# Token loads moved into the first half of layer 0's modulation weights, and small loads moved off the SP queue

## The chip, the cores and the metric

The kernel runs on one core of a Trainium2 chip. TensorE (PE) multiplies matrices, VectorE (DVE) and ScalarE (ACT) do elementwise work, GpSimd (POOL) does a few tiny operations, and SyncE (SP) issues most of the loads. Each engine works through its own list of instructions strictly in order. The metric is the time of one execution in microseconds on the device; less is better.

## The reference

Two transformer layers over 256 latent tokens `x` and 256 context tokens `ctx`, each of width 1024. Before each sub-layer a token row is normed and then modulated by vectors that come from a conditioning vector (`c` for latents, `c_ctx` for context):

```
mod_x = silu(c) @ ada_w[l] + ada_b[l]          # 6 * 1024 columns: shift, scale, gate, twice
hx    = modulate(rmsnorm(x, mix_pre_g[l]), shift, scale)
zx    = hx @ w_in[l]                           # then four mixing branches, SwiGLU, residuals
```

All is float32; a product is made in three passes of split operands. Nothing of the main work can start before the modulated tokens `hx`, `hc` of layer 0 are there, and these need both the normed tokens and `silu(c) @ ada_w[0]` for shift and scale (8 MB of weights).

## The kernel before

**The head.** `run` (L1114) starts with `setup`: it loads `c`, `c_ctx` and an identity matrix and makes `cs = silu(c)`. Then `ada_first` (L269) computes shift (j = 0) and scale (j = 1) of layer 0 for both streams. Its weights come as 16 loads of 512 KB, all issued by SP. The output columns are taken in two halves h (512 columns each), and within a half in pairs of k (128 rows of the contraction each); so a half is eight loads. The product over k is shared: all of j = 1 and the last k of j = 0 go to PE as `g<-ada,cs` (L301, 2 output rows by 512 columns, each recorded as two matmuls), the first `CUT` = 3 or 6 k of j = 0 go to DVE, which accumulates `acc` for both streams by `scalar_tensor_tensor` (L101). DVE then transposes `acc` in blocks (L332), sums the blocks to `vsum` (L333), and PE folds the four quarters (L339). ACT copies PE's rows out (`row`), PE transposes them, and DVE adds all up into the columns `adac`. The generator yields at its two ends of half.

**The tokens.** `load_x` brings `x` and `ctx` in as four loads of 512 KB. The table entry `XPOS` says after which (h, k) of the weights' loads they are issued: (1, 0), so after ten weight loads. For each of the four tiles of 128 tokens ACT squares the two halves of a row (`xs<-x`, with sums), DVE and POOL make the reciprocal root (`vn`, `rn`), and DVE scales the row, 512 columns at a time (`normed`, L413). PE transposes 128x128 blocks (`a<-ident,xs`, L179), and `modulated` (L431) applies shift and scale (`hm`) and splits the result in two parts, `h` on ACT and the rest on DVE. That is done for output half h = 0 first (k tiles 0 to 3), then for h = 1.

**What follows.** The first product of the main work is `g<-wh,h` (L170 to L172) with a unit of `w_in`, whose weights are split into `wh` (ACT) and `wl` (DVE). From then on the weights stream in by units.

**What sets the order.** The instructions are written by these generators, and a scheduler of the language then lays them in each engine's list; a wait holds everything behind it on that engine. Loads issued by SP and ACT take eight completion semaphores in turn, and a load that takes one again first waits for the load that had it; POOL's loads have eight others.

**The small loads.** `vectors(l)` (L212) loads eight vectors of a layer (`vin`, 85 rows of 128 numbers), issued by SP: for layer 0 after the fourth weight load, for layer 1 after the tables. `tables` (L231) loads the rotary tables `r` and the mask `mf` (320 KB), also by SP. `layer_consts` loads `gk`, `sink` and `wpl` by POOL.

Of the kernel before, what the change touches and what calls it, by code (L numbers as in the profile page):

```python
# [33 lines left out]
FILL = (2.0, 1.8)  # L34
RATE = (0.3, 0.45, 0.9, 1.0, 0.5)
CUT = (3, 6)
XPOS = (1, 0)
PUMP = ((0, 20, 2.5, 2.5, 7.5, 15), (15, 0, 30, 20, 2.5, 0))
NEG = -1e30

# [31 lines left out]
class Backbone:  # L72
# [138 lines left out]

    def vectors(self, l):  # L212

        d, c, g = self.d, self.const, self.nc.sync.dma_start
        vin = self.tp.tile([85, 128], F, tag=f"vin{l}", name="vin")
        row = lambda a: a[l].rearrange("(k p) -> k p", p=128)
        at = 0
        for name in ("mix_pre_g", "ffn_pre_g", "ada_b", "d_scale", "b_qa_g", "b_kva_g", "mix_post_g", "ffn_post_g"):
            r = row(d[name])
            g(vin[at:at + r.shape[0]], r)  # L220
            at += r.shape[0]
        yield
        ps = self.pa()
        self.tr(ps[:, 0:85], vin)
        col = c.tile([128, 85], F, tag=f"cols{l}", name="cols")
        self.act(col, ps[:, 0:85])
        self.cols[l] = dict(mix=col[:, 0:8], ffn=col[:, 8:16], ada=col[:, 16:64], ds=col[:, 64:66],
                            qa=col[:, 66:68], kva=col[:, 68:69], mixp=col[:, 69:77], ffnp=col[:, 77:85])
        yield

    def tables(self):  # L231
        nc, d, c, g = self.nc, self.d, self.const, self.nc.sync.dma_start
        t = lambda shape, name, dt=F: c.tile(shape, dt, name=name, tag=name)
        self.r64, self.r32 = t([128, 2, 128], "r64"), t([128, 2, 64], "r32")
        g(self.r64, d["rope64"])
        g(self.r32, d["rope32"])
        mf = self.tp.tile([128, 2, 128], F, tag="mf", name="mf")
        g(mf, d["mask"])
        self.mask, self.identb = t([128, 2, 128], "mask", BF), t([128, 128], "identb", BF)
        nc.vector.tensor_copy(self.mask, mf)  # L240
        nc.vector.tensor_copy(self.identb, self.ident)
# [27 lines left out]
    def ada_first(self, load, vec):  # L269


        w = self.d["ada_w"][0].rearrange("(k p) n -> p k n", p=128)
        raw = {}
        for h in range(2):
            for k in range(0, NK, 2):
                for j in range(2):
                    t = self.tp.tile([128, 2, 512], F, tag="ada", name="ada", bufs=16)
                    self.nc.sync.dma_start(t, w[:, k:k + 2, j * D + h * 512:j * D + h * 512 + 512])
                    raw[j, h, k], raw[j, h, k + 1] = t[:, 0], t[:, 1]
                if h == 0 and k == 2:  # L280
                    next(vec)
                if (h, k) == XPOS:
                    load()
        for j in range(2):
            for s in range(2):
                self.mod[0, j, s] = self.const.tile([128, NK], F, tag=f"ada0{j}{s}", name="adac")
        def add(j, h, x, y):
            c = slice(4 * h, 4 * h + 4)
            for s in range(2):
                o = self.mod[0, j, s][:, c]  # L290
                self.tt(o, x[:, :, s], o if y is None else y[:, c], ALU.add)

        v = self.vsums()
        for h in range(2):
            cut = (CUT[h], 0)
            ps = [self.pg() for j in range(2)]
            acc = [self.ap_.tile([128, 512], F, tag="acc", name="acc", bufs=2) for s in range(2)]
            for k in range(NK):
                for j in range(2):
                    if k >= cut[j]:  # L300
                        self.nc.tensor.matmul(ps[j][0:2], self.cs[:, :, k], raw[j, h, k], start=k == cut[j], stop=k == NK - 1)  # L301
                    else:
                        for s in range(2):
                            self.ada_step(acc[s], raw[j, h, k], s, k, self.ts)
            if h == 0:
                next(vec)
            for s in range(2):
                self.quad_sums(v[:, s, 16 * h:16 * h + 16], acc[s], raw[0, h, s])
            pv = self.pg()
            self.fold_quads(pv, v[:, :, 16 * h:16 * h + 16])  # L310
            add(0, h, pv[:, 0:8].rearrange("p (s k) -> p k s", s=2), self.cols[0]["ada"])
            for j in range(2):
                row = self.tp.tile([128, 512], F, tag="row", name="row", bufs=4)
                self.act(row[0:2], ps[j][0:2])
                x = pv[:, 8 + 8 * j:16 + 8 * j].rearrange("p (k s) -> p k s", s=2)
                for k in range(4):
                    self.tr(x[:, k], row[0:2, k * 128:(k + 1) * 128])
                add(j, h, x, self.cols[0]["ada"][:, NK:2 * NK] if j else None)
            yield
# [90 lines left out]
        return out  # L410


    def normed(self, x, ss, out):  # L413

        v = self.sm(1, "vn")
        self.ts(v, ss[:, 0:1], ss[:, 1:2], EPS, ALU.add, ALU.add)
        r = self.pow_half(v, 1, "n")
        for h in range(2):
            c = slice(h * 512, h * 512 + 512)
            self.ts(out[:, c], x[:, c], r)  # L420

    def turn_in(self, t, x, pss, ks):

# [423 lines left out]
    def mixer(self, l, xs, hs, streams):  # L847
        tc = self.tc
        with ExitStack() as st:
# [40 lines left out]
            def pump(t):  # L890
                run([t])
# [222 lines left out]
    def run(self):  # L1114
        tc = self.tc
        self.mod = {}
        xs, both = {}, (0, 1)
# [6 lines left out]
        with tc.tile_pool(name="start", bufs=1) as self.tp:  # L1124
            self.setup()
            self.cols = {}
            vec = [self.vectors(l) for l in range(LAYERS)]
            tmp = {s: [self.tp.tile([128, D], F, tag="xs", name="xs", bufs=4) for _ in range(2)] for s in both}
            first = self.ada_first(lambda: xs.update({s: self.load_x(s, self.nc.sync) for s in both}), vec[0])
            next(first)  # L1130
            for s in both:
                for t in range(2):
                    self.normed(xs[s][t], self.squares(xs[s][t], tmp[s][t]), tmp[s][t])
            next(first)
            for h in range(2):
                for s in both:
                    ab = self.ab(0, "mix", s, (slice(4 * h, 4 * h + 4),))
                    pss = {}
                    for t in range(2):
                        self.turn_in(t, tmp[s][t], pss, (4 * h, 4 * h + 2))  # L1140
                    self.modulated(s, pss, ab, self.H)
                if not h:
                    self.first_w = self.wunit(self.d["w_in"][0], C_U, 256)
            self.tables()
            self.layer_consts(0)
            for _ in vec[1]:
                pass
# [57 lines left out]
```

## Time and profile before

| | us |
|---|---|
| median of 3 runs | 1337.62 (1335.01 to 1339.58) |
| the profiled execution, its own time | 1333.19 |
| its span, first to last instruction | 1331.4 |
| PE busy in the span | 1282.5 (96%) |
| DVE busy | 988.6 (74%) |
| ACT busy | 681.7 (51%) |

The span and the 1.8 us around it make the execution's own time. Times in the rows count from the start of the span. A row of the timeline gives start, duration, engine, line, operation, output and inputs, and in brackets how long the engine had idled before it and what ended that. Rows of matmuls that follow each other closely overlap: a duration holds the way through the array, so the distance of two starts is what one costs.

### The profile page before, as it was taken

Reading aid. Unit: us, or ns where it says so; the run is one execution under the profiler, and the core shown is the slowest. Engines: PE = TensorE matmul, PEld = TensorE weight load, DVE = VectorE, ACT = ScalarE, POOL = GpSimd, SP = SyncE. Lnnn points to the kernel's source line nnn. Section 1 sums busy time; section 2 is a strip of 40 time slices with the busy share of each in tenths; the row PEclk is TensorE's granted clock in tenths of the full one; section 3 lists DMA queues with packets and bytes.
Section 4 is the critical chain, followed back from the end, with each engine's and each line's share of the span. In section 5 each row is a group of like instructions: output and inputs, shape, how many; then the busy total and the mean of one; then the engine's idle time right before and its main releaser. Section 6 shows DMA issues by size and latency. Waiting matters only on the chain.

```text
span 1331.4 us, 20465 instructions
## 1 busy us (share of the span) xinstructions
PE 1282.5 (96%) x7357; PEld 1086.9 (82%) x7357; DVE 988.6 (74%) x2114; ACT 681.7 (51%) x1553; POOL 48.7 (4%) x74
## 2 busy tenths in 40 slices
PE   5998999999999999999999999989899999999997
PEld 1777787888778878887788888889799998798996
DVE  4867688878999668888557664676887888785664
ACT  2545466646655535343244333454766667545552
POOL 1012000000000010000000000110000000000000
PEclk9999999999999999999999999999999999999999
DMA  8734432243244714565547553055332536577652
GB/s 291 235 110 115 127 87 64 69 138 94 74 127 154 250 48 134 183 190 167 173 151 220 167 174 119 22 169 175 96 111 72 151 111 213 161 244 214 179 178 87
DMA packets 150521, 194.50 MB, mean 146 GB/s; under 512 B 6682, under 2 KB 106324, under 8 KB 150164
## 3 DMA queue, kind: packets, MB, share of 16 engines
q1 hardware_dynamic: 149092, 188.73, 45.7%
q0 software_dynamic: 1312, 4.46, 1.2%
q8 instruction: 58, 0.95, 0.3%
q14 instruction: 43, 0.35, 0.1%
q10 hardware_dynamic: 16, 0.00, 0.0%
HBM read 192.12 MB, written 1.05 MB: 145 GB/s over the span
## 4 chain that ended last, share of the span: by engine, by line
PE 78%; DVE 7%; DMA 7%; ACT 4%; issue 2%; POOL 1%; SPq 0%; DVEq 0%; POOLq 0%; ACTq 0%
PE g L170 20%; PE g L171 20%; PE g L172 20%; DMA araw<-in_ada_w_dram 4%; PE a L179 3%; PE a L170 3%; PE a L172 3%; PE a L171 3%; PE a L652 2%; PE a L601 2%; DVE acc L101 2%; DVE wl L93 2%; ACT grp L90 1%; DVE grp L93 1%; DMA ada<-in_ada_w_dram 1%
## 5 line engine op out<-in xcount | busy, mean ns | idle before, releaser
L90 ACT ACTIVATE wh<-raw 128x512 fp32r<-128x512 f32 (+1 forms) x482 | 296.7, 626 | 312.5 <-PE g L171 167.0
L93 DVE TENSOR_TENSOR wl<-raw,wh 128x512 fp32r<-128x512 f32 (+1 forms) x482 | 323.8, 684 | 119.9 <-ACT wh L90 117.3
L170 PE MATMUL g<-h,wh 128*128 128x512 f32 (+1 forms) x1168 | 394.0, 338 | 3.9 <-ACT th L90 1.3
L171 PE MATMUL g<-h,wh 128*128 128x512 f32 (+1 forms) x1168 | 392.8, 337 | 0.0
L172 PE MATMUL g<-h,wl 128*128 128x512 f32 (+1 forms) x1168 | 392.3, 336 | 0.0
L170 PEld LDWEIGHTS g<-h,wh 128*128 128x128 f32 x1168 | 221.0, 190 | 28.4 <-ACT th L90 1.8
L172 PEld LDWEIGHTS g<-h,wl 128*128 128x128 f32 x1168 | 221.5, 190 | 21.6
L171 PEld LDWEIGHTS g<-h,wh 128*128 128x128 f32 x1168 | 221.5, 190 | 21.2 <-issue 0.4
L101 DVE SCALAR_TENSOR_TENSOR acc<-araw,cs,acc 128x512 f32<-128x512 f32 x224 | 162.1, 748 | 89.5 <-DMA araw<-in_ada_w_dram 67.1
L170 PE MATMUL g<-wh,h 128*128 128x256 f32 (+3 forms) x368 | 111.8, 305 | 1.7 <-ACT h L90 1.7
L172 PE MATMUL g<-wh,h 128*128 128x256 f32 (+3 forms) x368 | 111.0, 303 | 2.5 <-DVE h L93 2.5
L171 PE MATMUL g<-wl,h 128*128 128x256 f32 (+3 forms) x368 | 111.2, 303 | 0.5 <-DVE wl L93 0.5
L101 DVE SCALAR_TENSOR_TENSOR th<-th,g 128x512 f32<-128x512 f32 (+1 forms) x126 | 67.8, 559 | 11.1 <-PE g L172 6.8
L172 PEld LDWEIGHTS g<-wh,h 128*128 128x128 f32 x368 | 70.3, 191 | 4.4 <-DVE h L93 2.9
L170 PEld LDWEIGHTS g<-wh,h 128*128 128x128 f32 x368 | 70.3, 191 | 4.2 <-ACT h L90 2.2
L171 PEld LDWEIGHTS g<-wl,h 128*128 128x128 f32 x368 | 70.3, 191 | 2.3 <-DVE wl L93 0.7
L90 ACT ACTIVATE th<-g 128x512 f32<-128x512 f32 (+1 forms) x102 | 49.8, 492 | 38.0 <-PE g L172 37.3
L90 ACT ACTIVATE p<-a,nm 128x512 f32<-128x512 f32 (+1 forms) x72 | 44.2, 614 | 23.0 <-DVE nm L97 17.3
L170 PE MATMUL a<-wh,g 128*128 128x512 f32 x132 | 52.6, 399 | 1.1 <-DVE adac L93 1.1
L172 PE MATMUL a<-wh,g 128*128 128x512 f32 x132 | 52.2, 395 | 0.0
L171 PE MATMUL a<-wl,g 128*128 128x512 f32 x132 | 52.0, 394 | 0.0
L90 ACT ACTIVATE pth<-a 128x512 fp32r<-128x512 f32 (+1 forms) x72 | 37.8, 525 | 25.0 <-PE a L179 24.3
(228 smaller groups left out, 2000.9 us busy)
## 6 DMA issues: line engine op xcount, KB each, us to landing
raw<-in_w_ffn_dram SPq DMA_DIRECT2D x128, 512.0 KB
raw<-in_w_in_dram SPq DMA_DIRECT2D x84, 512.0 KB
araw<-in_ada_w_dram SPq DMA_DIRECT2D x80, 512.0 KB
ada<-in_ada_w_dram SPq DMA_DIRECT2D x16, 512.0 KB
raw<-in_w_branch_dram SPq DMA_DIRECT2D x32, 256.0 KB
raw<-in_w_out_dram SPq DMA_DIRECT2D x16, 512.0 KB
raw<-in_w_in_dram SPq DMA_DIRECT2D x8, 416.0 KB
band<-in_pool_dram POOLq DMA_DIRECT2D x2, 1024.0 KB, 7.9
```

What stands on the lines that cost most here:

```text
L90: return self.nc.scalar.activation(out, in_, func, **k)
L93: return self.nc.vector.tensor_tensor(out=out, in0=a, in1=b, op=op)
L101: return self.nc.vector.scalar_tensor_tensor(out=out, in0=a, scalar=s, in1=b, op0=op0, op1=op1)
L170: mm(ps, ah, bh, start=k == 0 and opens, stop=False, skip_group_check=True)
L171: mm(ps, ah, bl, start=False, stop=False, skip_group_check=True)
L172: mm(ps, al, bh, start=False, stop=last, skip_group_check=True)
L179: self.nc.tensor.transpose(out, in_, self.ident[0:k, 0:k])
L601: nc.tensor.matmul(ps[:, 0:nk], x, y, start=i == 0, stop=i == len(mms) - 1 and not masked)
L652: nc.tensor.matmul(po[:, 0:256], grp[:, 4, kts[k] * 128:kts[k] * 128 + 128], pt[j][:, k], start=j == 0 and k == 0, stop=j == 1 and k == n - 1)
```

## The change

`XPOS` becomes (0, 4): the tokens are loaded after six of the sixteen weight loads. `vectors` issues its loads from ACT for layer 0 and from POOL for layer 1, and is started before the first weight load; its transposed block takes a PSUM buffer of the other pool. `tables` issues its loads from POOL. `ada_first` yields once more, right after issuing its loads, and `run` now writes the four norms before the first half's products, and all transposes of a half before its last sums. In `normed` the second half of a row is scaled by ACT.

```diff
-XPOS = (1, 0)
+XPOS = (0, 4)
...
     def vectors(self, l):
-        d, c, g = self.d, self.const, self.nc.sync.dma_start
+        d, c, g = self.d, self.const, (self.nc.gpsimd if l else self.nc.scalar).dma_start
...
-        ps = self.pa()
+        ps = self.pg()
...
     def tables(self):
-        nc, d, c, g = self.nc, self.d, self.const, self.nc.sync.dma_start
+        nc, d, c, g = self.nc, self.d, self.const, self.nc.gpsimd.dma_start
...
     def ada_first(self, load, vec):
+        next(vec)
         for h in range(2):
...
-                if h == 0 and k == 2:
-                    next(vec)
                 if (h, k) == XPOS:
                     load()
+        yield
...
-    def normed(self, x, ss, out):
+    def normed(self, x, ss, out, by_act=()):
...
-            self.ts(out[:, c], x[:, c], r)
+            if h in by_act:
+                self.act(out[:, c], x[:, c], scale=r)
+            else:
+                self.ts(out[:, c], x[:, c], r)
...
-                    self.normed(xs[s][t], self.squares(xs[s][t], tmp[s][t]), tmp[s][t])
-            next(first)
+                    self.normed(xs[s][t], self.squares(xs[s][t], tmp[s][t]), tmp[s][t], (1,))
             for h in range(2):
+                pss = {s: {} for s in both}
                 for s in both:
-                    ab = self.ab(0, "mix", s, (slice(4 * h, 4 * h + 4),))
-                    pss = {}
                     for t in range(2):
-                        self.turn_in(t, tmp[s][t], pss, (4 * h, 4 * h + 2))
-                    self.modulated(s, pss, ab, self.H)
+                        self.turn_in(t, tmp[s][t], pss[s], (4 * h, 4 * h + 2))
+                next(first)
+                for s in both:
+                    self.modulated(s, pss[s], self.ab(0, "mix", s, (slice(4 * h, 4 * h + 4),)), self.H)
```

What this makes of the engines' lists is shown at three places; behind the first 150 or so rows of PE the lists are the same but for line numbers.

SP, from the first weight load to the token loads (`ada` are weights of shift and scale, `vin` the small vectors, `x` the tokens), before:

```order
L278 DMA ada<-in_ada_w_dram 128x2x512 x4
L220 DMA vin<-in_mix_pre_g_dram 8x128
L220 DMA vin<-in_ffn_pre_g_dram 8x128
L220 DMA vin<-in_ada_b_dram 48x128
L220 DMA vin<-in_d_scale_dram 2x128
L220 DMA vin<-in_b_qa_g_dram 2x128
L220 DMA vin<-in_b_kva_g_dram 1x128
L220 DMA vin<-in_mix_post_g_dram 8x128
L220 DMA vin<-in_ffn_post_g_dram 8x128
L278 DMA ada<-in_ada_w_dram 128x2x512 x6
L1021 DMA x<-in_x_dram 128x1024 x2
```

and of the changed kernel, from its first row on:

```order
L193 DMA cin<-in_c_dram 8x128
L195 DMA ident<-in_ident_dram 128x128
L279 DMA ada<-in_ada_w_dram 128x2x512 x6
L1024 DMA x<-in_x_dram 128x1024 x2
L1024 DMA x<-in_ctx_dram 128x1024 x2
L279 DMA ada<-in_ada_w_dram 128x2x512 x10
L132 DMA raw<-in_w_in_dram 128x4x256 x4
```

The `vin` rows have left SP's list, the tokens stand four loads earlier, and `w_in`'s units follow the weights without anything between.

DVE at the end of the second half's sums (`acc` up to `vsum`; `h` and `hm` are modulated tokens, `wl` split weights of `w_in`), before:

```order
L101 SCALAR_TENSOR_TENSOR acc<-ada,cs,acc 128x512
L97 TENSOR_SCALAR xs<-x,rn 128x512 x2
L101 SCALAR_TENSOR_TENSOR acc<-ada,cs,acc 128x512 x7
L332 STREAM_TRANSPOSE ada<-acc 128x512 x2
L333 TENSOR_REDUCE vsum<-ada 128x16 x2
L93 TENSOR_TENSOR h<-hm,h 128x256 x3
L98 TENSOR_SCALAR hm<-a,adac 128x256 x2
```

and of the changed kernel:

```order
L101 SCALAR_TENSOR_TENSOR acc<-ada,cs,acc 128x512
L93 TENSOR_TENSOR h<-hm,h 128x256 x2
L98 TENSOR_SCALAR hm<-a,adac 128x256
L101 SCALAR_TENSOR_TENSOR acc<-ada,cs,acc 128x512
L93 TENSOR_TENSOR h<-hm,h 128x256
L101 SCALAR_TENSOR_TENSOR acc<-ada,cs,acc 128x512 x3
L332 STREAM_TRANSPOSE ada<-acc 128x512
L93 TENSOR_TENSOR wl<-raw,wh 128x512 x2
L333 TENSOR_REDUCE vsum<-ada 128x16
L93 TENSOR_TENSOR wl<-raw,wh 128x512 x2
L332 STREAM_TRANSPOSE ada<-acc 128x512
L93 TENSOR_TENSOR wl<-raw,wh 128x512
```

The last `vsum` comes right behind these rows. Before, the modulation of the first half stood behind it, but for one `hm`; now all of that modulation (four `hm`, eight `h`) and five `wl` stand ahead of it.

PE from the token transposes to the first products of the main work, before:

```order
L179 MATMUL a<-ident,xs 128x128 x20
L301 MATMUL g<-ada,cs 2x512 x8
L339 MATMUL g<-vsum,quads 32x8 x4
L179 MATMUL a<-ident,xs 128x128 x4
L170 MATMUL g<-wh,h 128x256
L179 MATMUL a<-ident,xs 128x128 x2
L179 MATMUL g<-ident,row 128x2 x4
```

and of the changed kernel:

```order
L301 MATMUL g<-ada,cs 2x512 x2
L179 MATMUL a<-ident,xs 128x128 x4
L301 MATMUL g<-ada,cs 2x512 x3
L339 MATMUL g<-vsum,quads 32x8 x4
L179 MATMUL g<-ident,vin 128x85
L170 MATMUL g<-wh,h 128x256
L171 MATMUL g<-wl,h 128x256
L172 MATMUL g<-wh,h 128x256
L179 MATMUL g<-ident,row 128x2 x4
```

In both lists the fold of the second half (L339) stands ahead of the first `g<-wh,h`; the token transposes that stood behind the fold have moved ahead of it.

## Rows read from the trace of the kernel before

**Rows 1.** The page: busy time of the engines, share of the span and instructions
```profile
PE 1282.5 (96%) x7357; PEld 1086.9 (82%) x7357; DVE 988.6 (74%) x2114; ACT 681.7 (51%) x1553; POOL 48.7 (4%) x74
```
**Rows 2.** Windows: stretch, length, busy by engine, granted clock, DMA share, GB/s
```profile
10.00:16.00 6.00, 5.83 (x10) 0.92 (x10) 5.70 (x11) 0.00 (x0) 0.00 (x0) 1.00 0.46 147
18.00:34.00 16.00, 12.59 (x44) 4.39 (x41) 7.51 (x24) 8.34 (x23) 2.65 (x4) 0.88 1.04 410
38.00:44.00 6.00, 6.00 (x28) 1.96 (x27) 6.00 (x14) 2.45 (x6) 0.00 (x0) 1.00 0.60 162
50.00:60.00 10.00, 10.00 (x86) 10.00 (x86) 9.27 (x23) 9.50 (x25) 1.58 (x3) 1.00 0.57 165
```
**Rows 3.** Timeline of SP: the last small load and the next weights
```profile
13.21 0.27 SPq L220 DMA_DIRECT2D vin<-in_ffn_post_g_dram  x1
13.52 3.09 SPq L278 DMA_DIRECT2D ada<-in_ada_w_dram  x6
```
**Rows 4.** Timeline of ACT: the first square of tile 0 and of tile 1
```profile
25.38 0.63 ACT L90 ACTIVATE xs<-x 128x512 f32<-128x512 f32 x1 [0.24 <-DMA x<-in_x_dram]
...
26.66 0.63 ACT L90 ACTIVATE xs<-x 128x512 f32<-128x512 f32 x1
```
**Rows 5.** Timeline of DVE: second half's sums, and what stands between
```profile
22.80 0.88 DVE L97 TENSOR_SCALAR acc<-ada,cs 128x512 f32<-128x512 f32 x2 [5.17 <-DMA ada<-in_ada_w_dram]
24.89 0.23 DVE L93 TENSOR_TENSOR adac<-g,adac 128x4 f32<-128x4 f32 x2 [1.20 <-PE g L179]
...
27.64 0.88 DVE L97 TENSOR_SCALAR xs<-x,rn 128x512 f32<-128x512 f32 x2 [0.68 <-POOL rn L117]
...
33.54 0.88 DVE L97 TENSOR_SCALAR xs<-x,rn 128x512 f32<-128x512 f32 x2 [0.44 <-POOL rn L117]
34.34 4.72 DVE L101 SCALAR_TENSOR_TENSOR acc<-ada,cs,acc 128x512 f32<-128x512 f32 x7
38.98 1.30 DVE L332 STREAM_TRANSPOSE ada<-acc 128x512 f32<-128x512 f32 x2
40.20 1.24 DVE L333 TENSOR_REDUCE vsum<-ada 128x16 f32<-128x512 f32 x2
41.35 1.09 DVE L93 TENSOR_TENSOR h<-hm,h 128x256 fp32r<-128x256 f32 x3
42.35 1.00 DVE L98 TENSOR_SCALAR hm<-a,adac 128x256 f32<-128x256 f32 x2
...
55.50 1.29 DVE L93 TENSOR_TENSOR wl<-raw,wh 128x512 fp32r<-128x512 f32 x2
```
**Rows 6.** Timeline of PE in the head
```profile
17.48 7.03 PE L301 MATMUL g<-ada,cs 128*2 128x512 f32 x16 [0.39 <-DMA ada<-in_ada_w_dram]
...
25.57 1.88 PE L301 MATMUL g<-ada,cs 128*2 128x512 f32 x4
...
35.13 7.47 PE L301 MATMUL g<-ada,cs 128*2 128x512 f32 x15
42.01 0.24 PE L339 MATMUL g<-vsum,quads 128*32 128x8 f32 x6
...
47.70 0.60 PE L179 MATMUL a<-ident,xs 128*128 128x128 f32 x4
```
**Rows 7.** Windows of PE: stretch, length, PE busy, granted clock, DMA share, GB/s
```profile
30.00:31.00 1.00, 0.79 (x4) 0.54 1.05 406
...
36.00:37.00 1.00, 1.00 (x3) 0.54 1.09 388
...
122.00:123.00 1.00, 0.71 (x2) 0.62 0.97 268
...
125.00:126.00 1.00, 0.43 (x2) 0.67 0.84 263
```
**Rows 8.** DMA issues: size, us from issue to landing
```profile
gk<-in_a_kn_g_dram POOLq DMA_DIRECT2D x1, 32.0 KB, 6.9
sink<-in_c_sink_dram POOLq DMA_DIRECT2D x1, 2.0 KB, 7.8
```

## The prediction

> **What bounds the kernel now.** I read the page first: PE is busy 96% of the span [rows 1], so a change pays only where PE waits, or where it stands in front of PE's work. The change touches the head alone, so the windows came next. From 50 us on PE is busy without a gap, at the full clock [rows 2]; from there on a delay or a gain of the head moves everything behind it by the same amount, since the engines' lists behind the head are the same. Two windows show holes in the transfers: the DMA share is 0.46 from 10 to 16 and 0.60 from 38 to 44, against 1.04 and 410 GB/s between [rows 2]. The first hole is (1 - 0.46) x 6 = 3.2 us, and SP's timeline says why: the next weights are issued at 13.52, behind a `vin` row that was held until 13.21 [rows 3]. The second is (1 - 0.60) x 6 = 2.4 us.
>
> Then the engines' timelines of the head. The main work opens with `g<-wh,h`, and ahead of it in PE's list stands the fold of the second half's sums, at 42.01 [rows 6]. It waits for DVE's last `vsum`, which ends at 40.20 + 1.24 = 41.44 [rows 5]. From 34.34 on DVE goes from `acc` through the transposes to `vsum` without a gap [rows 5]. So DVE's list sets the start of the main work, and the reader should ask of the change: when does DVE reach that last `vsum`?
>
> **The change part by part.**
>
> *Transfers.* A 512 KB load takes 524 KB / 410 GB/s = 1.28 us [rows 2]. Before, the first tokens are the eleventh such load and ACT starts on them at 25.38 [rows 4]. Now they are the seventh: 4 x 1.28 = 5.1 earlier. The `vin` loads no longer hold SP: 3.2 earlier. The 320 KB of tables now run beside the first weights instead of behind them: 0.8 later at 410 GB/s. So the tokens begin at 25.4 - 5.1 - 3.2 + 0.8 = 17.9. The first half's last weights, the twelfth load, land at 17.9 + 5 x 1.28 = 24.3, the second half's first at 25.6, and the last at 34.5 instead of 36.9. The units of `w_in` follow at once, so the second hole goes too; but PE has its data then anyway, so that is worth nothing.
>
> *Norms.* Two squares cost ACT 26.66 - 25.38 = 1.28 per tile [rows 4]. ACT's half of the scaling isn't in the trace; DVE's half row takes 0.44 [rows 5], a square of that shape 0.63 [rows 4], I take 0.55. Four tiles make 4 x 1.83 = 7.3, and the last one's root adds the 27.64 - 26.66 = 1.0 that tile 0 shows [rows 4, 5]. The norms end near 17.9 + 7.3 + 1.0 = 26.2; ACT's part could move this by 0.4 either way.
>
> *DVE up to the last `vsum`.* The second half's `acc` now stand behind the norms: they start at 26.2, not at 22.80, though their data are there at 25.6. From there DVE's list holds: two first `acc` 0.88; ten more at 4.72 / 7 = 0.67, 6.7; three pairs of `adac` at 0.23, 0.7; four `hm` at 0.50, 2.0; eight `h` at 1.09 / 3, 2.9; two transposes 1.3; two sums 1.24; five `wl` at 0.645, 3.2 [rows 5]. That is 19.0. It also waits for the first half's columns from PE; before, that wait was 1.2 [rows 5], and I take the same, between 0 and the 5.2 that the first `acc` pair shows as a wait for data. So `vsum` ends at 26.2 + 19.0 + 1.2 = 46.4, against 41.44: **5.0 later**. The data that now come early do not help, since the work that filled the space behind the fold (`h`, `hm`, `wl`) has moved ahead of it.
>
> *PE behind the fold.* Twelve of the token transposes stood behind the fold and now stand ahead of it, in time in which PE waits: 3 x 0.60 = **1.8 earlier** [rows 6]. The modulation of the second half and its weights must be ready for PE's second 48 products; they have 48 x 10 / 86 = 5.6 us for it [rows 2], and before, with more of DVE's work left, PE had no gap in 50 to 60 [rows 2]. No cost.
>
> *The clock.* Before, the last four matmuls of the first product group start at 25.57 [rows 6]; then PE only transposes tokens, and the granted clock falls in the window 30 to 31 (0.54, so at 30.1) from 2.4 to 1.2 GHz. It is back in the window 36 to 37 (at 36.9) [rows 7], after products began again at 35.13 [rows 6]. Now the same stretch of transposes comes in the midst of the first half: the products of load six end near 18.3 (its data at 16.6, two products of 2 x 0.43 each), and the next stand behind the third tile's transposes, near 24.5. So I expect the fall there. The four products that follow are eight matmuls of 0.43 at full clock [rows 6] and 0.86 at half, and DVE waits for their columns: 0.9 lost if the clock returns as it did (15 matmuls took 7.47 where 16 took 7.03 [rows 6]), 3.4 if it does not. I take half of the eight: **1.7 later**. Then PE's last product ends near 40 and it idles until the fold at 46: the main work begins at half clock. The rows have 0.9 for such a return (the one above) and 1.7 (3.4 us at half between the windows 122 and 126 [rows 7]); I take **1.3 later**.
>
> A rule of the Trainium skill bears on this: "TensorE: Matmul & The Clock Gate", Part 4 on PE-mode transposes, says that transposes do not count for the clock as products do. The trace agrees as far as it goes: the half clock lasted through the token transposes. By that rule the sum is the one below; if transposes held the clock up, it would be the first rival's.
>
> *What I cost at nothing.* Eight `vin` loads on ACT: their issue stands in ACT's idle start, ahead of `cols` and the squares. But PE's transpose of `vin` now stands ahead of the products of loads four to six, and the last `vin` is issued only when the second weight load is down, near 13.2 - 2 x 1.28 = 10.6 [rows 3]. Six products, 5.2 us, follow, and load six lets them end at 18.3 at best: a landing until 13.1 is free. The nearest rows are POOL's, 6.9 and 7.8 from issue to landing [rows 8], which would cost 18.4 - 13.1 = 5.3; those queued behind each other, so I take 0 and keep 5.3. On DVE the mask's cast now waits for POOL's third load ahead of `cs`, which every product needs: with 7.8 [rows 8] that is near 10.5, when the second weights land too; up to 0.5, which PE wins back at 1.28 - 0.86 per load. The rotary products of DVE, 1.4, stand in the first half, where DVE waited 5.2 for data [rows 5]. Layer 1's `vin` on POOL is needed only near 46.
>
> **Sum.** 5.0 - 1.8 + 1.7 + 1.3 = 6.2 us slower: 1339.4 against the profiled execution's own 1333.2. That execution is 4.4 below the median, so on the scale of the median 1337.6 + 6.2 = **1343.8**.
>
> **Rivals.** (1) *The clock holds, or falls where nothing waits*: 5.0 - 1.8 = 3.2, 1340.8. For it: products and transposes are more mixed now than they were. Against it: the half clock of 30 to 37. (2) *Transfers decide after all*: DVE keeps up with the weights, so that the last `vsum` keeps its distance from the last weights. Then the head gains 2.4 of arrival and 1.8 of transposes, 4.2: 1333.4, faster. It decides if DVE needs under 13 us, not 20, between the norms and `vsum`, or if the tokens are there 7 us sooner; the rows give no such thing, but the order of rows that I sum is not yet a trace. (3) *The small loads land late*: a last `vin` at 16 instead of 13 holds PE, the first half's columns and the norms behind them on DVE by 3: 1346.8. The rows of POOL's loads speak for it, the small size against.
>
> **Chances.** The forecast 0.50, rival 1 0.25, rival 2 0.11, rival 3 0.14. What a measurement here can tell from no change is about 0.3%, 4 us. Rival 2 is faster (0.11). Rival 1 lies mostly within (0.22, and 0.03 beyond), and of the forecast, with small clock terms, 0.04: same 0.26. Slower: 0.46 + 0.03 + 0.14 = 0.63. The forecast's own range is 1341.4 to 1345.9 (clock terms 0.9 + 0.9 with the column wait at 0, to 3.4 + 1.7); for 8 in 10 I go from 1336.5 to 1349.5, which holds rivals 1 and 3 and leaves rival 2 out.
>
> **What would show it.** Right, if in the profile after the first square starts near 18, DVE's last `vsum` ends near 46 or later with DVE nearly without a gap from 27 on, PE waits for it, and the first `g<-wh,h` starts near 47 at half clock. The transfers' holes should be gone. Wrong, if `vsum` ends before 43, if the clock stays full between 20 and 50, or if the stretch behind 60 us changes its length by itself.

## The result, and the profile after

| | before | after |
|---|---|---|
| median of 5 runs of each, side by side | 1339.58 (1335.01 to 1340.08) | 1345.47 (1342.32 to 1346.55) |
| the profiled execution, its own time | 1333.19 | 1346.55 |
| its span | 1331.4 | 1344.4 |

The change makes the kernel slower: the ratio of the times is 1.0051, 95% interval 1.0030 to 1.0072, so 4 to 10 us. In a later comparison (e5 below) it was 1.0076 (1.0062 to 1.0089). The two profiled executions differ by 13.0 us of span, more than the medians do; where the rest of that comes from is told at the end of the experiments.

The windows of the transfers, as in [rows 2]:

```profile
10.00:16.00 6.00, 4.81 (x11) 0.66 (x9) 5.38 (x14) 0.24 (x1) 3.59 (x7) 1.00 0.95 333
38.00:44.00 6.00, 6.00 (x22) 1.77 (x20) 6.00 (x15) 3.77 (x10) 0.00 (x0) 1.00 0.32 103
50.00:60.00 10.00, 8.62 (x49) 8.07 (x50) 7.55 (x22) 5.23 (x12) 0.00 (x0) 0.52 0.74 206
```

In 10 to 16 the share is now 0.95 for 0.46. But the first hole has moved rather than closed. The stretch from 8 to 11 of before, the same of after, and SP's longest wait up to 16 us in after (who waits for what: us in total, times, longest):

```profile
8.00:11.00 3.00, 0.83 (x2) 0.14 (x3) 0.70 (x3) 0.00 (x0) 0.00 (x0) 1.00 0.99 345
```
```profile
8.00:11.00 3.00, 2.70 (x4) 0.34 (x4) 2.45 (x6) 0.00 (x0) 1.04 (x2) 1.00 0.73 152
```
```profile
SPq L279 <- DMA vin<-in_ada_b_dram: 5.9, 1, 5.9
```

From 8 to 11 the loads bring 152 GB/s for 345. SP's fifth weight load stands still for 5.9 until a small load that ACT had issued has landed, because the loads of SP and of ACT take the same eight completion semaphores in turn. The second hole has deepened (0.32 for 0.60): there SP's next load waits 10.5 for DVE's `wl`. In 50 to 60 PE was busy for 10.00 us at full clock before; now it is 8.62 at 0.52. So the loss sits ahead of 60 us. DVE's timeline, as in [rows 5] (start, duration, engine, line, operation, and in brackets the idle time before it and what ended it):

```profile
27.88 0.48 DVE L97 TENSOR_SCALAR xs<-x,rn 128x512 f32<-128x512 f32 x1 [0.66 <-POOL rn L117]
28.28 0.87 DVE L97 TENSOR_SCALAR acc<-ada,cs 128x512 f32<-128x512 f32 x2
...
34.29 0.23 DVE L93 TENSOR_TENSOR adac<-g,adac 128x4 f32<-128x4 f32 x2 [4.48 <-PE g L179]
...
35.58 0.23 DVE L93 TENSOR_TENSOR adac<-g,cols 128x4 f32<-128x4 f32 x2 [0.40 <-PE g L179]
...
46.35 1.25 DVE L93 TENSOR_TENSOR wl<-raw,wh 128x512 fp32r<-128x512 f32 x2
47.52 0.68 DVE L333 TENSOR_REDUCE vsum<-ada 128x16 f32<-128x512 f32 x1
...
50.51 0.67 DVE L333 TENSOR_REDUCE vsum<-ada 128x16 f32<-128x512 f32 x1
```

The norms end at 28.36. DVE then waits 4.48 + 0.40 for the columns that PE makes of the first half, and its last `vsum` ends at 50.51 + 0.67 = 51.18, not at 41.44. The `wl` rows between the transposes and the sums are work that stood behind the last `vsum` before. ACT's timeline, as in [rows 4]:

```profile
19.23 0.63 ACT L90 ACTIVATE xs<-x 128x512 f32<-128x512 f32 x1 [4.60 <-DMA x<-in_x_dram]
...
22.78 0.72 ACT L90 ACTIVATE xs<-x,rn 128x512 f32<-128x512 f32 x1 [0.38 <-POOL rn L117]
```

The tokens are squared from 19.23 on, 6.2 earlier than before, and ACT's half row of scaling takes 0.72, more than a square (0.63). PE's timeline, as in [rows 6]:

```profile
14.09 0.27 PE L179 MATMUL g<-ident,vin 85*128 85x85 f32 x1 [0.90 <-DMA vin<-in_ffn_post_g_dram]
...
26.18 1.12 PE L179 MATMUL a<-ident,xs 128*128 128x128 f32 x4 [1.74 <-DVE xs L97]
27.22 3.57 PE L301 MATMUL g<-ada,cs 128*2 128x512 f32 x4
30.73 1.11 PE L179 MATMUL a<-ident,xs 128*128 128x128 f32 x4
31.77 2.15 PE L301 MATMUL g<-ada,cs 128*2 128x512 f32 x4
33.85 0.41 PE L179 MATMUL g<-ident,row 2*128 2x2 f32 x4
...
51.23 0.30 PE L339 MATMUL g<-vsum,quads 128*32 128x8 f32 x8 [4.34 <-DVE vsum L333]
...
56.54 0.41 PE L172 MATMUL g<-wh,h 128*128 128x256 f32 x1
56.75 0.41 PE L170 MATMUL g<-wh,h 128*128 128x256 f32 x1
...
60.05 0.28 PE L172 MATMUL g<-wh,h 128*128 128x256 f32 x1
60.17 0.28 PE L170 MATMUL g<-wh,h 128*128 128x256 f32 x1
```

Between the tokens' transposes PE waits for DVE's scaled rows. The four matmuls at 27.22 take 3.57 where four took 1.88 before. PE then waits 4.34 for `vsum`, and the products of the main work stand 0.21 apart at 56.54 and 0.12 apart at 60.05. The granted clock in the token stretch, as in [rows 7]:

```profile
22.00:32.00 10.00, 8.03 (x21) 0.51 1.05 408
```

It is at its lower level (1.2 GHz) from 22.1 to 32.3 and from 49.4 to 59.6 (0.52 in 50 to 60, above), together 20.5 us against 6.8 before. For the whole head one row serves best as a mark, the first `pm` of ACT, behind 288 products of the main work. Of before, and of after:

```profile
81.27 0.38 ACT L90 ACTIVATE pm<-a 128x256 f32<-128x256 f32 x1 [0.49 <-PE a L808]
```
```profile
92.00 0.38 ACT L90 ACTIVATE pm<-a 128x256 f32<-128x256 f32 x1 [0.49 <-PE a L811]
```

The head is 10.7 us longer.

### The profile page after: what moved, and what is told of

Its sections match the earlier page's. It is cut to its first block, busy times and chain, and to the rows that moved or that the text cites. A ratio compares the mean times of both kernels' runs of the same rounds, so it can differ in the third digit from the quotient of the medians.

```text
span 1344.4 us, 20468 instructions
## 1 busy us (share of the span) xinstructions
PE 1290.7 (96%) x7357; PEld 1090.8 (81%) x7357; DVE 988.5 (74%) x2110; ACT 686.8 (51%) x1557; POOL 54.2 (4%) x85
## 4 chain that ended last, share of the span: by engine, by line
PE 79%; DVE 7%; DMA 6%; ACT 4%; issue 2%; POOL 1%; SPq 0%; DVEq 0%; POOLq 0%; ACTq 0%
PE g L170 21%; PE g L172 20%; PE g L171 20%; PE a L170 3%; PE a L179 3%; PE a L172 3%; PE a L171 3%; PE a L655 2%; PE a L604 2%; DMA araw<-in_ada_w_dram 2%; DVE acc L101 1%; ACT grp L90 1%; DMA raw<-in_w_in_dram 1%; DVE wl L93 1%; DVE grp L93 1%
## 5 line engine op out<-in xcount | busy, mean ns | idle before, releaser
L170 PE MATMUL g<-wh,h 128*128 128x256 f32 (+3 forms) x368 | 113.6, 309 | 2.2 <-ACT h L90 1.8
L172 PE MATMUL g<-wh,h 128*128 128x256 f32 (+3 forms) x368 | 112.6, 306 | 2.6 <-DVE h L93 2.6
L170 PEld LDWEIGHTS g<-wh,h 128*128 128x128 f32 x368 | 71.8, 195 | 4.7 <-ACT h L90 2.3
L172 PEld LDWEIGHTS g<-wh,h 128*128 128x128 f32 x368 | 71.7, 195 | 4.4 <-DVE h L93 3.0
```

The source lines that it names most:

```text
L170: mm(ps, ah, bh, start=k == 0 and opens, stop=False, skip_group_check=True)
L172: mm(ps, al, bh, start=False, stop=last, skip_group_check=True)
```

## The experiments

Ratios are to the kernel before, timed on the same chip between the runs of the experiment (before: medians 1332.6 to 1333.8 in the three comparisons). `vsum` is the end of DVE's last one in the head, `pm` the mark, "half" the time at 1.2 GHz ahead of 100 us, and behind it without the last 6 us of the kernel; these are of the one profiled execution.

| | median | ratio | `vsum` | `pm` | half, head | half, later |
|---|---|---|---|---|---|---|
| before (the first profile) | | 1 | 41.4 | 81.3 | 6.8 | 6.8 |
| after (the first profile) | 1345.5 | 1.0051 (1.0030 to 1.0072) | 51.2 | 92.0 | 20.5 | 10.2 |
| e1 loads only | 1333.9 | 1.0008 (0.9994 to 1.0021) | 41.3 | 81.2 | 6.8 | 13.7 |
| e2 tokens only | 1342.7 | 1.0067 (1.0045 to 1.0088) | 50.5 | 91.2 | 13.7 | 6.8 |
| e3 sums first | 1333.2 | 0.9988 (0.9978 to 0.9998) | 43.5 | 83.1 | 6.8 | 3.4 |
| e4 PE kept busy | 1335.3 | 1.0012 (1.0001 to 1.0023) | 48.6 | 86.4 | 0 | 13.7 |
| e5 after, again | 1341.5 | 1.0076 (1.0062 to 1.0089) | 50.9 | 91.7 | 17.1 | 6.8 |
| e6 sums first, PE busy | 1331.7 | 0.9992 (0.9981 to 1.0002) | 41.3 | 80.9 | 0 | 17.1 |
| e7 `wl` behind `vsum` | 1339.9 | 1.0063 (1.0049 to 1.0077) | 47.2 | 90.2 | 13.7 | 3.4 |
| e8 scaling on DVE | 1340.4 | 1.0062 (1.0049 to 1.0075) | 49.4 | 89.8 | 13.7 | 6.8 |
| e9 e3 and e8 | 1333.8 | 1.0002 (0.9991 to 1.0014) | 42.2 | 81.7 | 3.4 | 3.4 |
| e10 e9, PE busy | 1330.3 | 0.9975 (0.9961 to 0.9990) | 40.9 | 80.4 | 0 | 6.8 |

**e1, the small loads alone.** The kernel before with:

```diff
-        d, c, g = self.d, self.const, self.nc.sync.dma_start
+        d, c, g = self.d, self.const, (self.nc.gpsimd if l else self.nc.scalar).dma_start
...
-        nc, d, c, g = self.nc, self.d, self.const, self.nc.sync.dma_start
+        nc, d, c, g = self.nc, self.d, self.const, self.nc.gpsimd.dma_start
...
+        next(vec)
         for h in range(2):
...
-                if h == 0 and k == 2:
-                    next(vec)
```

> The kernel before, with one part of the change alone: the vectors' small loads are issued by ACT and POOL and the tables' by POOL; the tokens stay where they were, behind the second half's first weights. Theory A (the start of the main work is set by what stands on DVE ahead of the second half's last `vsum`, and by TensorE's half clock in the token stretch; the small loads cost nothing): the hole of 3.2 us in the transfers closes, DVE's order stays as before, so the last `vsum` comes 0 to 2.4 us earlier than before (39 to 41.5), and the time is 1337 to 1340 beside 1339.6 before. Rival B (the small loads on the new queues are what costs: a late `vin` row and a cast that holds DVE): most of the 5.9 us of the whole change shows here, 1343 or more. Rival C (the half clock alone): no loss unless the half-clock stretches grow; 1339 to 1341.

No change that can be measured (1.0008), so the new place of the small loads costs nothing and rival B falls. It brings nothing either. SP waits here too, 6.0 for the same `vin<-in_ada_b` as in after, and ACT's timeline of e1 says where the rest of the gain ends:

```profile
24.26 0.63 ACT L90 ACTIVATE xs<-x 128x512 f32<-128x512 f32 x1
...
30.20 0.56 ACT L90 ACTIVATE hm<-a,adac 128x256 f32<-128x256 f32 x1 [2.04 <-PE a L179]
30.66 0.62 ACT L90 ACTIVATE xs<-x 128x512 f32<-128x512 f32 x1
```

The first square starts at 24.26, 1.1 earlier than before. But the last tile's squares stand in ACT's list behind an `hm` of the first tiles, which waits until 30.20 for PE's transposes, and start at 30.66, where they started at 30.87. `vsum` ends at 41.29, as before.

**e2, the tokens alone.** The kernel after, with the diff of e1 undone.

> The other part alone: tokens in the middle of the first half, norms and modulation ordered as in the kernel after, with one half of each scaling on ACT; the small loads stay on SP where they were. Theory A: the loss is here. The norms and the last `vsum` come as late as in the kernel after (51.2) or up to 2.4 us later, since the hole in the transfers is back: 1345 to 1349, slower than before by 5 to 9. Rival B: within 2 us of before, 1338 to 1342. Rival C: as after, 1344 to 1347, with DVE's work from the norms to the last `vsum` no longer than the 12 us that its sums need at full clock.

The loss is here (+0.67%), with `vsum` at 49.81 + 0.68 = 50.49. DVE needs 21.9 us from the norms to there, which C excluded. Theory A put it at or behind after's 51.2; it came 0.7 earlier: in e2's list four `wl` stand ahead of it and not five, and the wait for the columns was 3.89. The tokens arrive at the same time as in after:

```profile
19.17 0.63 ACT L90 ACTIVATE xs<-x 128x512 f32<-128x512 f32 x1 [2.18 <-DMA x<-in_x_dram]
```

So beside the moved tokens the small loads' new place brought no gain (19.23): what the stretch from 10 to 16 won had been lost ahead of it. Besides SP's wait of 5.9, the DMA queues of e2 and of after from 5 to 12 us show a loss (queue: packets, MB, share of the 16 engines' time; q0 is POOL's, q1 holds SP's weights):

```profile
q1 hardware_dynamic: 1072, 1.90, 71.3%
q0 software_dynamic: 199, 0.10, 17.8%
```
```profile
q1 hardware_dynamic: 798, 1.53, 59.3%
q0 software_dynamic: 258, 0.30, 38.3%
```

With the tables on POOL's queue, 0.30 MB of small loads take 38.3% of the engines' time, where 0.10 MB took 17.8%, and the weights come down to 1.53 MB from 1.90. How much of that is SP's wait and how much POOL's queue, no run parts. The Trainium skill ("DMA: Bandwidth & Descriptors", section "SWDGE vs HWDGE vs iDMA") says that POOL's and SP's transfers feed different queues of an engine and that the engine takes them in turn. The trace agrees as far as it goes: both queues move in the same stretch, and q1's share falls while q0's rises; the turns themselves it does not show.

**e3, the order of the second half.** After, with the second half's sums written ahead of the first half's modulation:

```diff
+            pss = [{s: {} for s in both} for h in range(2)]
             for h in range(2):
-                pss = {s: {} for s in both}
-                for s in both:
-                    for t in range(2):
-                        self.turn_in(t, tmp[s][t], pss[s], (4 * h, 4 * h + 2))
+                if not h:
+                    ...
                 next(first)
+            for h in range(2):
+                if h:
+                    ...
                 for s in both:
-                    self.modulated(s, pss[s], ...
+                    self.modulated(s, pss[h][s], ...
```

> The kernel after, with the second half's sums moved ahead of the first half's modulation in the program; loads, tokens and norms as in after. Theory A: four `hm`, most of eight `h` and five `wl` (8.1 us of DVE) leave the stretch ahead of the last `vsum`, which ends near 42 to 44 instead of 51.2; the modulation and the weights then stand behind the fold as they did before, so not all of it comes back: the main work begins 3 to 6 us earlier than in after, 1340 to 1342.5. Rival B: the small loads are as in after, so nothing comes back: 1345. Rival C: the token stretch and PE's wait ahead of the fold are still there, so the clock falls as in after: 1344 to 1346 though `vsum` is earlier.

The whole loss goes: 0.12% under the kernel before. DVE's timeline of e3 behind the norms:

```profile
33.35 0.23 DVE L93 TENSOR_TENSOR adac<-g,adac 128x4 f32<-128x4 f32 x2 [3.49 <-PE g L179]
...
34.99 2.73 DVE L101 SCALAR_TENSOR_TENSOR acc<-ada,cs,acc 128x512 f32<-128x512 f32 x4
...
38.43 2.73 DVE L101 SCALAR_TENSOR_TENSOR acc<-ada,cs,acc 128x512 f32<-128x512 f32 x4
41.07 1.30 DVE L332 STREAM_TRANSPOSE ada<-acc 128x512 f32<-128x512 f32 x2
42.30 1.24 DVE L333 TENSOR_REDUCE vsum<-ada 128x16 f32<-128x512 f32 x2
```

The `acc` now stand together, and one `hm` and one `h` are left among them. `vsum` ends at 43.54, 7.6 earlier than in after, with the tokens' half clock and the wait for PE's columns (3.49 + 0.40) still there. The mark is 8.9 earlier; mark and time both come back by more than A expected. C falls: the same stretch of transposes, the same kind of wait, and the loss is gone. PE waits only 1.39 at once ahead of the fold, and the clock does not fall a second time.

**e4, PE kept busy.** After, with every engine's list in the head held in the order of after by a table, and products that nobody reads:

```diff
+    def warm(self, name, n, out, rhs):
+        for _ in range(n):
+            i = self.nc.tensor.matmul(out, self.cs[:, :, 0], rhs, start=True, stop=True)
...
     def turn_in(self, t, x, pss, ks, warm=("", 0), by=None):
...
+            self.warm(*warm, o, by[:, 0:256].rearrange("p (i c) -> p i c", i=2))
...
-            pv = self.pg()
+            pv = self.pg(); self.warm(f"f{h}", 6 * h, pv[0:2], raw[0, h, 2])
```

> The kernel after with the order of every engine's list in the head held as it is (a table), and products of no use put into PE's waits: nine of 2x256 between the fold of the first half and the third tile's transposes, six of 2x512 ahead of the second fold. Their results are overwritten unread. Theory A: the granted clock stays full from 12 us on; DVE's wait for PE's columns falls from 4.9 to 1 to 2, the last `vsum` comes near 47 to 48, still 6 later than before, and the first 31 products of the main work take 0.12 and not 0.21 us: 4 to 6 us come back of the profile's 13, so 1340 to 1342. Rival C: the half clock is all of it: the last `vsum` ends by 43 and the time is that of before or less, 1336 to 1340. Rival B, or a clock that doesn't follow PE's products: no change, 1345, and a half clock in the same places.

The clock stays full through the head, in the windows of e4:

```profile
22.00:32.00 10.00, 9.32 (x41) 1.00 1.05 407
50.00:59.00 9.00, 9.00 (x76) 1.00 0.62 183
```

and the wait for the columns, `vsum`, the first half's last products and the fold, on DVE and on PE of e4, are:

```profile
31.70 0.23 DVE L93 TENSOR_TENSOR adac<-g,adac 128x4 f32<-128x4 f32 x2 [1.59 <-PE g L179]
...
47.92 0.67 DVE L333 TENSOR_REDUCE vsum<-ada 128x16 f32<-128x512 f32 x1
```
```profile
27.05 1.88 PE L301 MATMUL g<-ada,cs 128*2 128x512 f32 x4
28.86 0.66 PE L179 MATMUL a<-ident,xs 128*128 128x128 f32 x4
29.45 1.88 PE L301 MATMUL g<-ada,cs 128*2 128x512 f32 x4
31.26 0.41 PE L179 MATMUL g<-ident,row 2*128 2x2 f32 x4
...
48.65 0.24 PE L339 MATMUL g<-vsum,quads 128*32 128x8 f32 x6
```

The wait is 1.59 + 0.40 = 2.0 for 4.9. `vsum` ends at 48.59, still 7.2 later than before: that part is the norms and DVE's order and not the clock, as A has it. The mark comes 5.6 earlier than in after, within what was expected; by the ratios (1.0012 against 1.0051 and, in e5, 1.0076) 5 to 8.5 us come back. So in time the busy PE alone takes back most of the loss, and the order alone (e3) all of it: the order removes the late `vsum` and with it the second fall of the clock, the busy PE removes both falls and leaves the mark 5.2 behind that of before. The Trainium skill ("TensorE: Matmul & The Clock Gate", Part 4) says that transposes do not keep the clock up as products do. The trace agrees as far as it goes: in after the clock fell at 22.1, at the first of the tokens' transposes (22.04) and behind 2.40 of idling, and with nine products set among the same transposes it held. The products filled idle time too, so no run here parts the transposes from the waits between them.

**e5, after again.**

> The kernel after, unchanged, on the same chip as the other experiments of this call, so that they stand beside it. Theory A has it 5 to 9 us slower than the kernel before (ratio 1.004 to 1.007), with DVE's last `vsum` at 50 to 51.5 and the half clock in the token stretch and at the start of the main work. A rival in which most of the 5.9 us belongs to the place of the first comparison expects a ratio under 1.003.

The ratio, 1.0076, is a little over the range; `vsum` at 50.22 + 0.69 = 50.91 and two half-clock stretches as in after (25.1 to 32.0 and 49.0 to 59.3). So the loss is no accident of the first comparison.

**e6, e3 and the busy PE.** The table of e4 with the order of e3, nine products of no use among the first transposes, none ahead of the fold.

> The second half's sums ahead of the first half's modulation (as in e3), and nine products of no use between the fold of the first half and the third tile's transposes (as in e4), the order of e3 held by a table. If the order on DVE and the half clock are two costs that add up: DVE's wait for PE's columns falls from 3.5 to 1.3 to 2, the last `vsum` from 43.5 to 41 to 42, and the main work is 2 to 2.5 us earlier than in e3: 2 to 4.5 us under the kernel before (ratio 0.9965 to 0.9985). If the clock only mattered through the order that e3 has mended, as e3: ratio 0.998 to 1.0.

In the profile the two add up: the wait is 1.59 + 0.40, `vsum` ends 2.2 and the mark 2.2 earlier than in e3. In the times they do not: 0.9992 against 0.9988, though the two intervals overlap. Its profile has 17.1 us of half clock behind 100 us, against 3.4 in e3; but it shows the slowest of e6's eleven runs, and by the runs' mean clocks (median 0.995, and 0.993 in e3) both kernels have some 8 to 10 us there. So the later stretches do not explain it.

**e7, less work ahead of `vsum`.** After, with the table, and five `wl` of DVE behind the last `vsum`; rows of DVE's list:

```diff
 STREAM_TRANSPOSE ada<-acc 128x512
-TENSOR_TENSOR wl<-raw,wh 128x512 x2
 TENSOR_REDUCE vsum<-ada 128x16
-TENSOR_TENSOR wl<-raw,wh 128x512 x2
 STREAM_TRANSPOSE ada<-acc 128x512
-TENSOR_TENSOR wl<-raw,wh 128x512
 TENSOR_REDUCE vsum<-ada 128x16
-TENSOR_TENSOR wl<-raw,wh 128x512
+TENSOR_TENSOR wl<-raw,wh 128x512 x6
```

> The kernel after with one engine's list changed by a table: the five `wl` that DVE has ahead of the last `vsum` (3.2 us) stand behind it; every other list stays. The reading that the last `vsum` alone sets the time expects 3 us back: `vsum` near 48, and 2.5 to 3 us under after. The other reading, that the products need those `wl` too, so that DVE's work is only moved behind the fold, expects `vsum` near 48 and the first product 3 us earlier, but the products then wait for DVE's `wl` (0.64 each, while an `wl` serves twelve products of 0.12 to 0.21): the 96th product within 1 us of after, and the time within 1.5 us of it.

`vsum` ends at 47.22, 4.0 earlier than in after, and the first product starts at 47.78. But then PE stands:

```profile
47.78 0.36 PE L170 MATMUL g<-wh,h 128*128 128x256 f32 x1
...
51.02 0.58 PE L179 MATMUL g<-ident,row 2*128 2x2 f32 x4 [2.65 <-DVE adac L93]
```

Three products, and then 2.65 of waiting for an `adac` that now stands behind the `wl`. The mark is 1.5 to 1.9 earlier than in the two profiles of after, the ratio 1.0063 against 1.0076. That lies between the two readings and nearer the second, since 0.6 to 0.7 of it is a shorter wait for PE's columns (3.75 for 4.48 and 4.38). "The last `vsum` sets the time" was too short: what counts is all that DVE must do until PE can run on, and that e3 gains because its sums fill time in which DVE had waited is my reading of its rows, not a run of its own.

**e8, the scaling back on DVE.** After, with `self.normed(..., tmp[s][t])` and no `(1,)`.

> The kernel after with both halves of each token tile's scaling on DVE, as before the change. ACT's half row takes 0.72 us in the trace of after where a square takes 0.63 and DVE's half row 0.48. Taking it off ACT shortens ACT's chain of four tiles by 2.9, and puts 4 x 0.40 = 1.6 more on DVE, which waited for the norms: they end 0.5 to 1.5 us earlier than 28.4, if ACT's chain sets them. The last `vsum` is then 0 to 1.5 us earlier, the time 0 to 1.5 us under after. Theory A expects no more than that, since what stands on DVE behind the norms stays; the rival that the norms on ACT are what costs expects 4 us or more.

The norms end at 27.5 for 28.4, `vsum` at 49.43, 1.5 to 1.8 earlier than in the two profiles of after; 1.0062. The order behind the norms is what costs, not the norms on ACT.

**e9 and e10, both edits, and both with the busy PE.** e9 is the diff of e3 and that of e8; e10 sets eight products of no use among its first transposes.

> The two edits that each gave time back, together: the second half's sums ahead of the first half's modulation (e3), and both halves of the scaling on DVE (e8). If they add up, the norms end near 27.4 instead of 28.4, the last `vsum` near 42 to 42.5 instead of 43.5 and the 96th product near 57.5: 1 us under e3, so 2 to 3.5 us under the kernel before (ratio 0.9975 to 0.9985). If in e3's order PE's products and not the norms decide by then, as e3 (0.9985 to 0.9995).

> e9 with eight products of no use (2x256 each) in PE's waits between the fold of the first half and the third tile's transposes. If the head's gain is kept to the end: the last `vsum` near 40.5 to 41.5, the 96th product 1 to 2.5 us earlier than in e9 and the ratio 0.996 to 0.998. If, as the runs of e6 suggest, part of what the head gains at the full clock is lost to stretches of half clock behind 100 us, the ratio is within 0.0005 of e9's, and the profile shows the 96th product earlier all the same, with more half clock behind 100 us than e9.

e9's mark is 1.3 earlier than e3's, as expected, but its time is not (1.0002). e10 is faster than both kernels, 0.25% (0.10% to 0.39%) under before and, by the two ratios of after, 0.8% to 1.0% under after. Its last sum:

```profile
39.61 1.24 DVE L333 TENSOR_REDUCE vsum<-ada 128x16 f32<-128x512 f32 x2
```

**What lies behind the head.** A half-clock stretch can also come at places far behind it. Two windows of PE of after:

```profile
486.00:490.00 4.00, 4.00 (x15) 0.57 0.47 131
902.00:907.00 5.00, 4.26 (x20) 0.66 0.15 52
```

After has three such stretches, at 486, 903 and 1159, before two, at 122 [rows 7] and 1146. Instructions of the same name and number, taken in both traces, show what they do: after is 10.7 late at the mark, 9.3 behind 126, 9.9 at 469, 11.5 at 491, 11.0 at 891, 12.7 at 918 and 13.1 at the end. So the stretches at 486 and 903 took 1.6 each from after; those at 1146 and 1159 stand at the same instructions and change nothing between the two.

The 1.1 that comes back between 104 and 126 is not the stretch at 122. DVE waits there for `gk`, a small load of POOL's, and PE, further on, for DVE's `m`. Before, and after:

```profile
110.45 1.03 DVE L93 TENSOR_TENSOR rg<-gk,r 128x128 f32<-128x128 f32 x6 [5.33 <-DMA gk<-in_a_kn_g_dram]
...
126.16 0.50 PE L170 MATMUL g<-o,wh 128*128 128x512 f32 x1 [0.73 <-DVE m L101]
```
```profile
119.74 1.03 DVE L93 TENSOR_TENSOR rg<-gk,r 128x128 f32<-128x128 f32 x6 [4.21 <-DMA gk<-in_a_kn_g_dram]
...
135.48 0.51 PE L170 MATMUL g<-o,wh 128*128 128x512 f32 x1 [2.10 <-DVE m L101]
```

`gk` comes 9.3 later in after, where the head is 10.4 late, and everything behind it is 9.3 late. The products that before ran at half clock at 122 only shorten PE's next wait, 0.73 for 2.10: that stretch cost nothing.

The mean clock that each run records tells how much half clock there is in all: it is 0.996 in the median of e4's runs and 0.990 in e5's, 10.7 and 26.8 us at half clock by (1 - clock) x 2 x time. The head has 0 and 17.1 of these, so the rest is about equal, 10 us. In e9's runs it is 0.992, 21 us, though its profiled execution has 0.996. Within a kernel the times follow this clock: e9's two runs at 0.996 took 1331.1 and 1331.9, its four at 0.991 took 1333.7 to 1335.5. A straight line through the 159 runs of the three later comparisons, with a level of its own for each kernel and comparison, gives 0.27 us for each us at half clock (an estimate). At equal clock it puts after (e5) 8.2 us behind the kernel before and e4 4.4, each give or take about 1, and e3, e6, e9 and e10 within 1 us of it. So the little that e3 and e10 gain over before is for the most part clock: in e10 the head's 6.8 us that are now at full clock, in e3, whose head has as much half clock as before's, what fell to its runs further on. Why e6 and e9 do not show the gains that their marks have over e3's is left open.

## Why the prediction was right, and where its sizes were off

The time (1345.5 for 1343.8), the sign and the mechanism on DVE and PE held: DVE's list makes `vsum` late, PE waits for it, and the main work starts at half clock. The step on the transfers failed, and three of the four terms came out too small. That the total came within 1.7 us is in part luck: at the mark the sum was 4.5 short, and of the 10.7 us there only 5.9 (first comparison) to 9.0 (e5) reached the medians. The fold, 42.01 before, 51.23 in after and 48.65 in e4, and the mark behind it part them (e4 differs from after in the products of no use alone; the third line holds whatever else differs between fold and mark):

| term | predicted | in the profiles |
|---|---|---|
| `vsum` by DVE's list, clock aside | +5.0 | +6.6 (48.65 - 42.01) |
| half clock on the first half's products | +1.7 | +2.6 (51.23 - 48.65) |
| transposes moved ahead of the fold | -1.8 | -1.5 (fold to mark: 37.79 in e4, 39.26 before) |
| main work at half clock | +1.3 | +3.0 (fold to mark: 40.77 in after, 37.79 in e4) |
| sum at the mark | +6.2 | +10.7 |

*Transfers.* The tokens were to be squared from 17.9 on and are from 19.23. What failed is "the `vin` loads no longer hold SP: 3.2 earlier": off SP's list, they hold it through the semaphores that it shares with ACT, 5.9 for one 24 KB load. With the 0.8 for the tables that term stood at 2.4; it brought 1.1 alone (e1) and nothing beside the moved tokens (e2, 19.17). The loads' place, taken as 5.1, brought 5.0 (24.26 in e1, 19.23 in after) to 6.2 (before, e2). The second hole, which was to go, grew.

*Norms.* I took 0.55 for ACT's half row; it takes 0.72. With the 1.3 of the tokens the norms end at 28.4 and not at 26.2. That is more than what is missing in the first line; DVE's work, below, gave some of it back.

*DVE up to `vsum`.* From the norms 18.0 of work, predicted 19.0; the sum by rows held. The wait for PE's columns, taken as 1.2, is 2.0 at full clock (e4) and 4.9 at half. And the step "`vsum` sets the start" is only half of it (e7).

*The clock.* The place of the first fall was right, and so, nearly, was half of the eight matmuls at half clock: between their starts in after and in e4 (27.22 to 30.73 for 27.05 to 28.86, 31.77 to 33.85 for 29.45 to 31.26) lie 2.0 us, for the 1.7 taken. What the sum put at nothing is the two groups of transposes ahead of and between them, 1.04 each for 0.59, 0.9 together; PE came to the first of these 0.3 earlier than in e4, and the whole is 2.6. The second fall came too; it lasted 10.2 us, where the dearer of the two rows that I took its price from had 3.4. That row had no price at all, as the waits behind 122 show above.

*What I cost at nothing.* The last `vin` held PE for 0.90 (at 14.09), nothing that reached the end (e1); so rival 3 was right in kind and wrong in price: it is SP that the late small loads held, and e1 shows no time lost by it (1.0008). DVE waited for the mask until 7.87, and the first product still started earlier than before, at 8.3 for 10.2. Rival 1 falls by the windows, rival 2 by `vsum`: DVE needed 22.9 us between the norms and `vsum`, not 13.

That the medians of the first comparison differ by 5.9 and not by 10.7 is not explained by any of these terms. Before's runs were 1335 to 1340 there and 1330 to 1338 in all later comparisons; after's profiled execution was its slowest, before's faster than all its timed runs. In e5 profile and runs agree better: 10.4 late at the mark, 8.0 at the end, and 9.0 by the medians. What comes back behind the mark, 2.4 there, comes back in e3 too (1.8 late at the mark, 0.4 early at the end); about 1 of it is the wait for `gk`, 5.33 in before and 4.38 and 4.52 in e5 and e3.

## What to carry to other kernels

When loads are moved to another engine's queue, look at what the old queue waits for then: here the hole from 10 to 16 us came back from 8 to 11, since SP and ACT share completion semaphores. And ask which engine's list takes an earlier transfer up: the tokens came 1.1 earlier in e1, and lists in fixed order waited elsewhere. When work is moved into a stretch in which an engine waits, look at what it is put in front of: the same loads and norms cost 0.8% with the second half's sums behind the modulation (e5) and nothing (-0.1%) with them ahead of it (e3). And where PE has only transposes and waits, count what follows at half clock, or give it products.

## What the runs showed of the hardware

- Products that nobody reads, about 4 us of matmul rows among three groups of transposes, kept the granted clock at 2.4 GHz through the token stretch (e4, e6, e10), in which it fell in all nine other profiles.
- The landing of a 24 KB load issued by ACT held SP's next 512 KB load for 5.9 us, since the two took the same completion semaphore. Up to 24 us SP waited for none of the loads of POOL, which take eight others.
- POOL's small loads are not free to the others: 0.30 MB of them took 38.3% of the DMA engines' time from 5 to 12 us, where 59.3% carried 1.53 MB for SP. The mask, 128 KB, took 5.3 us from its issue to its landing.
- ACT's scaling by a per-row factor took 0.72 us for 128x512, its square with a sum 0.61 to 0.63, DVE's scaling 0.48.
- A stretch of half clock far behind the head cost 1.6 us at 486 and at 903 in after, and nothing at 122 in before, where PE had to wait anyway. The profiles of kernels whose lists are alike there have one to four such stretches, of 3.4 to 10.2 us.
